# Products on their own PSUM bank, and earlier operands, in a two-layer encoder trunk

## The chip, the cores and the metric

The kernel runs on one core of a Trainium2 chip. The metric is device microseconds (us) of one execution. The kernel before takes 1584.87 us, the median of 3 runs (1580.16 to 1585.47).

## The reference

A stream of 16 learned meta tokens and 512 frames, 1024 wide, goes through two layers in float32. Cut to what matters:

```python
h = concat(meta, x)                                        # 528 tokens
h = h + retention_mixer(rmsnorm(h), w_in, gn, w_o)         # layer 0: 4 heads, chunks of 64
h = h + (silu(n @ w1) * (n @ w3)) @ w2                     # n = rmsnorm(h); w1, w3: 1024x2816
kv_a = rmsnorm(h, g_kv) @ w_kv_a                           # 512 latent + 64 rotary key
k, v = up-projection of rmsnorm(kv_a[:512]) @ w_kv_b       # 8 heads, 128 + 64 rotary; v 128
q = rope(rmsnorm(rmsnorm(h) @ w_q_a) @ w_q_b)              # rank 768, 8 heads
h = h + (softmax(mask(q k^T)) @ v) @ w_o                   # block-causal, chunks of 64
h = h + (silu(n @ w1') * (n @ w3')) @ w2'                  # layer 1's feed-forward
return rmsnorm(h)[frames]
```

## The kernel before

**Layout and precision.** Activations lie transposed, features on the 128 partitions and tokens along the row: 528 of them (`T`) in the first layer and in the keys and values, 512 in the second layer's query side and feed-forward. Each operand is split in a high and a low half: `split` is a ScalarE copy (L316) and a VectorE subtraction (L312, the line of every `tt`), and `weights` does it for a block of weights that SyncE (SP) loads. Each product is three matmuls (high·high, high·low, low·high).

**Feed-forward** (`ffn`, `quads`; 76 quads). A 2x2 block product is done with seven products instead of eight. A *quad* is one such block with tokens cut in halves of `w` = 264 or 256 columns: an `Up` makes a pair of column blocks of w1 and w3 (12 matmuls a product), a `Down` adds one of four parts of w2 into the stream (3 matmuls for each of its `size` hidden pairs; `PARTS`, L48, lists the sizes). A layer has 38 quads, 8 Up, 4 Down (part 0), 8 Up, 4 Down, 6 Up, 4 Down, 4 Down. The products Q1 to Q7 accumulate in the four banks of one PSUM tile, `b0` or `b1`, in turn (L918). Sums of products are formed where they lie: ScalarE copies a bank into another (L833) before a product is added to it, and copies Q5's bank into `q5` (L887); `combine` (VectorE) adds q5 to two banks; `mid`, `act` and `fin` finish. In an Up, `mid` and `fin` multiply by 1/rms and by SiLU; in a Down they add to `h`, and in the last part of layer 1 also the squares for the final norm.

`period(i)` (L855) overlaps quad `i` (`q`), the one before (`prev`) and the loads of the next two; the order in which it issues is forced on every engine (L908 to L913). TensorE's order in it is Q1(q), Q7(prev), Q3(prev), Q5(q), Q6(q), Q4(prev), Q2(q). Four combinations of weights are made per quad: SP loads four parts raw (`load1` to `load4`), GpSimd adds with two accumulating DMAs (L801, L804), VectorE subtracts (`sum2` L807, `sum4`), and `group` splits two at a time: r1 for Q1 and Q5, r2 for Q6 and Q2, r3 for Q7 and Q3, and `group4` one for Q4. `hidden(i)` makes the next Down operand (`operands`, L760) in two halves in two successive periods, as `room` allows. `start` in period 0 takes the layer's root of the mean square.

**Second layer's attention** (`mla`, L977). First `prep_mla(k)` for each of 8 blocks of `h`: the scaled, split operands of the key-value branch and of the query branch, and a square added to a sum; then `gemm` of w_kva (5 blocks of 48 matmuls, first 528 columns), then w_qa, the first keys, values and queries. Eight heads follow; each has four blocks of scores, softmax and one `values`. Between a head's steps a `Filler` issues steps of other projections, in the order of the dictionary `order`, as many as `FILL` (L56) says: `query` (qN), `keys_values` (kvN, two heads), `rotary`, `project` (pN, output projection of two heads). Tiles come from a pool of slots (`MLA_SLOTS`, L46) and PSUM has four tiles for all of it (`pp`). After the last `project` the pools are shut, new ones opened, and `prep_ffn(1, k)` for 8 blocks makes the operands of layer 1's feed-forward.

```python
def product(q, bank, p, first):          # L824; the matmul is L829
nc.scalar.copy(out=q.q5, in_=q.ps[:, 3, :w])             # L887
for k in range(KD): self.prep_ffn(1, k)                  # in run(), after mla
```

Of the kernel before, what the change touches and what calls it, by code (L numbers as in the profile page):

```python
# [19 lines left out]
P = 128  # L20
D = 1024
# [23 lines left out]
RET_SLOTS = 45  # L45
MLA_SLOTS = 53  # L46

PARTS = (3, 3, 3, 2)  # L48

# [39 lines left out]
class Head:  # L89


    def __init__(self, k, n, kn, v, vi, qn, qr, krh, krl):
        self.k, self.nc = k, k.nc
# [53 lines left out]
    def values(self):  # L147
        k, nc = self.k, self.nc
        po = k.ps()
        c = slice(self.vi * P, (self.vi + 1) * P)  # L150
        for j in range(4):
            vh, vl = (u[:, c] for u in self.v[j])
            q0 = min(j, 2) * P
            ph, pl = (z[j // 2][:, j % 2, q0:] for z in (self.ph, self.pl))
            for t, (x, y) in enumerate(((vh, ph), (vh, pl), (vl, ph))):
                nc.tensor.matmul(po[:, q0:SEQ], x, y, start=j == 0 and t == 0, stop=False)  # L156
        nc.tensor.matmul(po[:, :SEQ], self.v[4][:, c], self.pm[:, :SEQ], start=False, stop=True)
        hi, lo = k.slot(F32R), k.slot(F32R)
        k.split(hi[:, :SEQ], lo[:, :SEQ], po[:, :SEQ])
        return hi, lo  # L160


class Quad:
# [7 lines left out]

    def mid(self, c1):
        pass
# [8 lines left out]
class Up(Quad):  # L182
# [11 lines left out]

    def mid(self, c1):
        self.t = self.k.temp()
        self.k.tt(self.two(self.t), c1, self.two(self.k.r), ALU.mult)

# [15 lines left out]
class Down(Quad):  # L214
# [12 lines left out]

    def add(self, i, c, op):
        k, h = self.k, self.h(i)
        k.tt(h, *((c, h) if op == ALU.add else (h, c)), op)  # L230
        if self.done and not self.full:
            m = 2 * self.o + i
            k.square_add(k.acc[:, :SEQ], k.h[m][:, META:], m == 0)

    def mid(self, c1):
        self.add(0, c1, ALU.add)

    def fin(self, c2):
        self.add(1, c2, ALU.subtract)


class Kernel:
# [112 lines left out]

    def gemm(self, src, m0, nm, x, full, chunk_k=8, evac=None, mid=None, mid_at=0):


        nk = len(x)
        for m in range(m0, m0 + nm):  # L360
            ps = self.ps()
            for k0 in range(0, nk, chunk_k):
                k1 = min(nk, k0 + chunk_k)
                hi, lo = self.weights(src[m][:, k0 * P : k1 * P], (k1 - k0) * P)
# [56 lines left out]
    def run(self):  # L421
# [19 lines left out]
        self.shut("pp", "yp")  # L441
        self.ffn(0, True)
        self.metas("mm", 4)
        self.pp = self.pool("pp", bufs=4, space=PSUM)
        self.sp = self.pool("sp", bufs=MLA_SLOTS)
        self.mla()
        self.shut("pp", "sp", "mm")
        self.wx = self.pool("wx")
        self.xp = self.pool("xp", bufs=4)
        for k in range(KD):  # L450
            self.prep_ffn(1, k)
        self.ffn(1, False)
# [11 lines left out]

    def prep(self, k, name, acc, full):

        v = self.h[k] if full else self.h[k][:, META:]
        n = T if full else SEQ
        hi, lo = self.slot(F32R), self.slot(F32R)
        self.split_scaled(hi[:, :n], lo[:, :n], v, self.g(name, k))  # L470
        if acc is not None:
            self.square_add(acc[:, :n], v, k == 0)
        return hi, lo

    def prep_ffn(self, layer, k):
# [10 lines left out]
        if k % 2:  # L486
            self.x.extend(self.operands(self.xp, self.vv, n // 2))

    def prep_mla(self, k):
        if k == 0:  # L490
            self.x, self.xq = [], []
        self.x.append(self.prep(k, "kv", self.acc, True))
        self.xq.append(self.prep(k, "mix1", None, False))

    def retention(self):
# [22 lines left out]
        for k in range(KD):  # L518
            c = slice(k % 4 * P, (k % 4 + 1) * P)
            x.append(self.prep(k, "mix0", None, True))  # L520
            for ps, z in zip(pk + pq, w):
# [254 lines left out]
    def quads(self, seq, w, start, hidden):  # L776
# [47 lines left out]
        def product(q, bank, p, first):  # L824
            wt = q.f[p]
            for k, xp in enumerate(q.xs()):
                cs = slice(k * P, (k + 1) * P)
                for i, (u, v) in enumerate(((0, 0), (0, 1), (1, 0))):
                    nc.tensor.matmul(q.ps[:, bank, :w], wt[u][:, cs], xp[:, p, v, :w], start=first and k == 0 and i == 0,  # L829
                                     stop=False, skip_group_check=True)  # L830

        def copy(q, to, of):
            nc.scalar.copy(out=q.ps[:, to, :w], in_=q.ps[:, of, :w])  # L833

# [17 lines left out]
        def combine(q):  # L852
            self.tt(q.ps[:, 1::2, :w], q.ps[:, 1:3, :w], q.q5[:, None, :].to_broadcast([P, 2, w]), ALU.add)

        def period(i):  # L855
            q, nxt, far = (seq[j] if j < len(seq) else None for j in range(i, i + 3))
            prev = seq[i - 1] if i else None
            if q:
                q.ps = self.pp4[i % 2]
                product(q, 0, Q1, True)  # L860
                group(q, q.r2, Q6, Q2)
                if far:
                    load1(far)
                copy(q, 1, 0)
            if prev:
# [3 lines left out]
                hidden(i)  # L869
                product(prev, 2, Q7, False)  # L870
                product(prev, 1, Q3, False)
                combine(prev)
                prev.mid(prev.ps[:, 0:2, :w])
            if nxt:
                sum2(nxt)
            if q:
# [4 lines left out]
                if nxt:  # L881
                    sum4(nxt)
                product(q, 3, Q5, True)
                if i == 0:
                    start()
                q.q5 = self.temp()[:, :w]
                nc.scalar.copy(out=q.q5, in_=q.ps[:, 3, :w])  # L887
            if nxt:
# [3 lines left out]
            if q:  # L892
                product(q, 1, Q6, False)
                copy(q, 2, 1)
            if prev:
                prev.act()
                product(prev, 2, Q4, False)
                prev.fin(prev.ps[:, 2:4, :w])
            if far:
                add3(far)  # L900
            if q:
                product(q, 0, Q2, False)

# [11 lines left out]
    def ffn(self, layer, full):  # L915
        nc, a = self.nc, self.a
        pool = self.pool("bk", bufs=1, space=PSUM)
        self.pp4 = [pool.tile([P, 4, 512], F32, tag=f"b{i}", name=f"b{i}_{layer}") for i in range(2)]  # L918
        w = HT if full else SEQ // 2
        n = 2 * w  # L920

        for z in self.pp4:
            for j in (1, 2):
                nc.tensor.matmul(z[:, j, :w], self.ones_r, self.x[0][:, 0, 0, :w], start=True, stop=False,
# [12 lines left out]
        def start():  # L937
            root(self.pp4[1][:, 3])
            nc.scalar.activation(out=acc, in_=r[:, :n], func=AF.Copy, scale=-1.0)
# [5 lines left out]
        for part, size in enumerate(PARTS):  # L945
# [4 lines left out]
            if part == 2:  # L950
                room += [(self.xp, len(seq) + 1)] * PARTS[3]
            for o in range(KD // 2):
# [15 lines left out]
        if not full:  # L968
            root(self.pp4[0][:, 0])
            for k in range(KD):  # L970
# [6 lines left out]
    def mla(self):  # L977
        nc, a = self.nc, self.a
        for k in range(KD):
            self.prep_mla(k)  # L980
        acc, xkv, xq = self.parted(self.acc, True), self.x, self.xq
        r = self.r
# [24 lines left out]
        def evac_q(m, ps):  # L1007
# [4 lines left out]

        drain(self.gemm(a["w_kva"], 0, 5, xkv, True, evac=evac_kv,
                        mid=partial(self.rstd, r, acc, D, self.eps_rms[:, 0:1], True)))
        ckv, cq = [], []
# [23 lines left out]
        def keys_values(pr):  # L1039
# [3 lines left out]
            for i in range(2):  # L1043
                ps = self.ps()
                for k in range(4):
                    c = slice((i * 4 + k) * P, (i * 4 + k + 1) * P)
                    self.mm(ps, (whi[:, c], wlo[:, c]), ckv[k], k == 0, k == 3, True)
                hi, lo = self.slot(F32R), self.slot(F32R)
                self.split(self.two(hi), self.two(lo), self.halves(ps))
# [22 lines left out]
        def project(pairs, g):  # L1072
# [4 lines left out]
            for m in range(4 * g, 4 * g + 4):  # L1077
# [6 lines left out]
                hv = self.h[m][:, META:]  # L1084
                self.tt(hv, ps[:, :SEQ], hv, ALU.add)
                yield

# [5 lines left out]
        for i, _ in enumerate(norm):  # L1093
            if i % 2:
# [54 lines left out]
    def mla_values(self, pr, ckv, out):  # L1149

        w = self.weights(self.a["w_kbv"][pr])
        w = [[u[:, k * 256 : (k + 1) * 256] for u in w] for k in range(4)]
        v = [(self.slot(F32R), self.slot(F32R)) for _ in range(2)]
        for j in range(5):
# [122 lines left out]
```

## Time and profile before

| | |
|---|---|
| median of 3 runs | 1584.87 us |
| profiled execution | 1589.51 us |
| its span, first to last instruction | 1587.5 us |
| mean granted TensorE clock | 0.973 of full |
| layer 0's retention; its feed-forward | to 477; 477 to 868 |
| second layer's attention; its feed-forward | 868 to 1165; to the end |

PE is the matmul engine TensorE, PEld its weight loads, DVE VectorE, ACT ScalarE, POOL GpSimd, SP SyncE. A row of a timeline has a start in us, the mean duration of one instruction in us, engine, line and operation, output<-input by the program's names, shapes, the count that is taken together, and in brackets the idle time before and what released it. An instruction's duration holds more than its turn: the next often starts before its end, so prices of a chain are read from start to start.

### The profile page before, as it was taken

The numbers are of one execution on the slowest core, as the hardware profiler recorded it, in microseconds if no ns is written. First come the engines' busy times: TensorE is split into PE (matmuls) and PEld (weight loads), VectorE is DVE, ScalarE is ACT, GpSimd is POOL, SyncE is SP. The second block draws the span as 40 slices with busy tenths as digits, with TensorE's granted clock in tenths as the row PEclk, the third lists the DMA queues.
The fourth block names the chain that finished last, engine by engine and source line by source line (L and its number), as shares of the span: only waits on it lengthen the run. The fifth ranks groups of instructions, "written<-read, shape, count | busy, mean of one in ns | idle before, by whom it ended". The sixth has DMA issues, their size and how long they took to land. (4 is left out here: it accounts for less than half of the span.)

```text
span 1587.5 us, 27865 instructions
## 1 busy us (share of the span) xinstructions
PE 1460.8 (92%) x10988; PEld 1388.9 (87%) x10988; DVE 1180.5 (74%) x1825; ACT 774.6 (49%) x1365; POOL 152.4 (10%) x196
## 2 busy tenths in 40 slices
PE   8999999999988999999997999989969999999984
PEld 8999999999977999999986988878859998989974
DVE  7585484575595888878888677676786878878876
ACT  6452442433464555545546446555464555545543
POOL 2000000000001111111111000000011111111110
PEclk9999999999998999999999899999979999999997
DMA  6222222132134667667655223212135676676651
GB/s 212 74 69 92 63 94 68 66 93 81 54 86 112 167 145 183 152 166 177 157 128 152 68 92 100 60 47 64 51 85 136 156 169 171 150 179 175 147 122 67
DMA packets 84802, 183.87 MB, mean 116 GB/s; under 512 B 9776, under 2 KB 30384, under 8 KB 84672
## 3 DMA queue, kind: packets, MB, share of 16 engines
q1 hardware_dynamic: 60336, 141.13, 28.2%
q0 software_dynamic: 24336, 40.98, 15.6%
q8 instruction: 86, 1.41, 0.4%
q14 instruction: 44, 0.36, 0.1%
HBM read 178.65 MB, written 2.10 MB: 114 GB/s over the span
## 5 line engine op out<-in xcount | busy, mean ns | idle before, releaser
L829 PE MATMUL b<-xp,whi 128*128 128x264 f32 (+1 forms) x3696 | 699.6, 290 | 77.8 <-ACT t L887 54.7
L829 PEld LDWEIGHTS b<-xp,whi 128*128 128x128 f32 x3696 | 579.4, 192 | 106.2 <-ACT t L887 71.2
L316 ACT CAST whi<-raw 128x1024 fp32r<-128x1024 f32 (+5 forms) x428 | 364.8, 856 | 403.0 <-PE b L829 197.6
L829 PE MATMUL b<-xp,wlo 128*128 128x264 f32 (+1 forms) x1848 | 528.0, 286 | 5.4 <-DVE wlo L312 5.4
L312 DVE TENSOR_TENSOR wlo<-raw,whi 128x1024 fp32r<-128x1024 f32 (+5 forms) x428 | 418.0, 980 | 120.5 <-ACT whi L316 116.8
L829 PEld LDWEIGHTS b<-xp,wlo 128*128 128x128 f32 x1848 | 354.4, 192 | 5.6 <-DVE wlo L312 5.6
L352 PE MATMUL ps<-s,whi 128*128 128x264 f32 x1824 | 303.9, 289 | 12.4 <-ACT whi L316 6.8
L352 PEld LDWEIGHTS ps<-s,whi 128*128 128x128 f32 x1824 | 258.2, 192 | 14.7 <-ACT whi L316 6.8
L352 PE MATMUL ps<-s,wlo 128*128 128x264 f32 x912 | 187.8, 288 | 0.0
L352 PEld LDWEIGHTS ps<-s,wlo 128*128 128x128 f32 x912 | 143.8, 192 | 0.1
L801 POOL DMA_DIRECT2D raw<-w x76 | 66.0, 868 | 772.4 <-DMA raw<-w 373.7
L354 PE MATMUL ps<-s,whi 128*128 128x512 f32 x368 | 117.3, 400 | 2.2 <-DVE s L312 1.4
L622 PE MATMUL ps<-whi,s 128*128 128x256 f32 x640 | 116.2, 281 | 0.4 <-DVE s L312 0.4
L833 ACT COPY b<-b 128x264 f32<-128x264 f32 (+1 forms) x152 | 54.7, 360 | 120.0 <-PE b L829 119.8
L312 DVE TENSOR_TENSOR s<-ps,s 128x256 fp32r<-128x256 f32 (+4 forms) x96 | 51.9, 558 | 73.0 <-ACT s L316 51.5
L622 PEld LDWEIGHTS ps<-whi,s 128*128 128x128 f32 x640 | 99.1, 188 | 0.9 <-DVE s L312 0.7
L804 POOL DMA_DIRECT2D raw<-w x76 | 65.7, 864 | 276.5 <-DMA raw<-w 167.9
L622 PE MATMUL ps<-wlo,s 128*128 128x256 f32 x320 | 89.5, 280 | 0.0
L354 PEld LDWEIGHTS ps<-s,whi 128*128 128x128 f32 x368 | 67.0, 188 | 17.7 <-DVE s L312 2.3
L312 DVE TENSOR_TENSOR xp<-e,xp 128x256 fp32r<-128x256 f32 (+5 forms) x90 | 68.1, 786 | 7.2 <-ACT xp L316 7.2
L354 PE MATMUL ps<-s,wlo 128*128 128x512 f32 x184 | 72.6, 395 | 0.0
L312 DVE TENSOR_TENSOR b<-b,t 128x528 f32<-128x528 f32 (+1 forms) x76 | 53.5, 704 | 24.8 <-PE b L829 24.8
(151 smaller groups left out, 1548.8 us busy)
## 6 DMA issues: line engine op xcount, KB each, us to landing
raw<-w SPq DMA_DIRECT2D x140, 256.0 KB, 3.8
raw<-w SPq DMA_DIRECT2D x44, 512.0 KB, 4.9
raw<-w POOLq DMA_DIRECT2D x88, 256.0 KB, 5.1
raw<-w SPq DMA_DIRECT2D x72, 192.0 KB, 3.2
raw<-w SPq DMA_DIRECT2D x24, 384.0 KB, 3.8
raw<-w POOLq DMA_DIRECT2D x48, 192.0 KB, 3.8
raw<-w_v SPq DMA_DIRECT2D x16, 512.0 KB, 3.8
raw<-w_g SPq DMA_DIRECT2D x16, 512.0 KB, 3.4
```

The costliest lines, as they stand in the source:

```text
L312: self.nc.vector.tensor_tensor(out=out, in0=a, in1=b, op=op)
L316: self.nc.scalar.copy(out=hi, in_=src)
L352: mm(ps[:, h * 512 : h * 512 + HT], w[p], x[q][:, h * HT : (h + 1) * HT], start=s, stop=e)
L354: mm(ps[:, :SEQ], w[p], x[q], start=s, stop=e)
L622: mm(ps[:, :256], x[k][p][:, c], w[k][q], start=k == 0 and i == 0, stop=k == last and i == 2)
L801: nc.gpsimd.dma_start(out=q.r1[:, 1], in_=q.part(3), accum_op=ALU.add)
L804: nc.gpsimd.dma_start(out=q.r3[:, 0], in_=q.part(0), accum_op=ALU.add)
L829: nc.tensor.matmul(q.ps[:, bank, :w], wt[u][:, cs], xp[:, p, v, :w], start=first and k == 0 and i == 0, stop=False, skip_group_check=True)
L833: nc.scalar.copy(out=q.ps[:, to, :w], in_=q.ps[:, of, :w])
```

## The change

In the feed-forward: the first product's bank becomes a tile of its own (`a{i}`), the other three (`b`, `d`, `c`) one tile; the order on TensorE becomes Q1(q), Q7(prev), Q3(prev), Q5(q), Q2(q), Q6(q), Q4(prev), with Q2 now accumulating in the first bank after the copy out of it; `mid` becomes two instructions, one for each bank; `PARTS` becomes (3, 3, 2, 3), with the room of the last two operands unchanged in number.

In attention: the first weights of w_kva are made ahead, then the key-value operands of all 8 blocks, then the squares; the query branch's operands are made two blocks at a time between w_kva's blocks. `yp`, a pool of 8 slots, holds first four query-branch operands, then keys and values of pair 0, then values of heads 2 and later; the common pool has 45 slots for 53. The fillers have another order. The pools of layer 1's feed-forward are opened before the last two projections, and each of their steps that completes a block of `h` calls `prep_ffn` for it.

```diff
-MLA_SLOTS = 53
+MLA_SLOTS = 45
...
-PARTS = (3, 3, 3, 2)
+PARTS = (3, 3, 2, 3)
...
# Head.values
-        hi, lo = k.slot(F32R), k.slot(F32R)
+        pool = k.yp if self.n >= 2 else None
+        hi, lo = k.slot(F32R, pool), k.slot(F32R, pool)
...
# Up.mid; Down.mid likewise
-    def mid(self, c1):
+    def mid(self, c11, c12):
         self.t = self.k.temp()
-        self.k.tt(self.two(self.t), c1, self.two(self.k.r), ALU.mult)
+        for i, c in enumerate((c11, c12)):
+            cs = slice(i * self.w, (i + 1) * self.w)
+            self.k.tt(self.t[:, cs], c, self.k.r[:, cs], ALU.mult)
...
# run
+        self.yp = self.pool("yp", "right", 8)
...
-        self.shut("pp", "sp", "mm")
-        self.wx = self.pool("wx")
-        self.xp = self.pool("xp", bufs=4)
-        for k in range(KD):
-            self.prep_ffn(1, k)
+        self.shut("pp", "yp")
         self.ffn(1, False)
...
# quads
-            self.tt(q.ps[:, 1::2, :w], q.ps[:, 1:3, :w], q.q5[:, None, :].to_broadcast([P, 2, w]), ALU.add)
+            self.tt(q.ps[:, 0::2], q.ps[:, 0:2], q.q5[:, None, :].to_broadcast([P, 2, w]), ALU.add)
...
# period(i)
-                q.ps = self.pp4[i % 2]
-                product(q, 0, Q1, True)
+                a, ps = self.banks[i % 2]
+                q.a, (q.b, q.d, q.c), q.ps = a[:, :w], (ps[:, j, :w] for j in range(3)), ps[:, :, :w]
+                product(q, q.a, Q1, True)
                 group(q, q.r2, Q6, Q2)
...
-                copy(q, 1, 0)
+                nc.scalar.copy(out=q.b, in_=q.a)
...
-                product(prev, 2, Q7, False)
-                product(prev, 1, Q3, False)
+                product(prev, prev.d, Q7, False)
+                product(prev, prev.b, Q3, False)
                 combine(prev)
-                prev.mid(prev.ps[:, 0:2, :w])
+                prev.mid(prev.a, prev.b)
...
-                product(q, 3, Q5, True)
+                product(q, q.c, Q5, True)
                 if i == 0:
                     start()
                 q.q5 = self.temp()[:, :w]
-                nc.scalar.copy(out=q.q5, in_=q.ps[:, 3, :w])
+                nc.scalar.copy(out=q.q5, in_=q.c)
...
-                product(q, 1, Q6, False)
-                copy(q, 2, 1)
+                product(q, q.a, Q2, False)
+                product(q, q.b, Q6, False)
+                nc.scalar.copy(out=q.d, in_=q.b)
             if prev:
                 prev.act()
-                product(prev, 2, Q4, False)
-                prev.fin(prev.ps[:, 2:4, :w])
+                product(prev, prev.d, Q4, False)
+                prev.fin(prev.ps[:, 1:3])
             if far:
                 add3(far)
-            if q:
-                product(q, 0, Q2, False)
...
# ffn
-                room += [(self.xp, len(seq) + 1)] * PARTS[3]
+                room += [(self.xp, len(seq) + 1)] * 2
...
# mla
-            self.prep_mla(k)
+        first = [self.weights(a["w_kva"][0])]
+        xkv = [self.prep(k, "kv", True) for k in range(KD)]
+        xq = []
+        for k in range(KD):
+            self.square_add(self.acc, self.h[k], k == 0)
...
+        for m, _ in enumerate(self.gemm(a["w_kva"], 0, 5, xkv, True, evac=evac_kv, ready=first,
+                                        mid=partial(self.rstd, r, acc, D, self.eps_rms[:, 0:1], True))):
+            for k in range(2 * m, min(2 * m + 2, KD)):
+                xq.append(self.prep(k, "mix1", False, self.yp if k < 4 else None))
...
# project, after the sum into h
+                if 3 in pairs:
+                    self.prep_ffn(1, m)
...
-        order = {"q2": query(2), "kv2": keys_values(2), "q3": query(3), "r1": rotary(1), "q4": query(4),
-                 "p0": project([0], 0), "p0b": project([0], 1), "q5": query(5), "kv3": keys_values(3), "q6": query(6),
+        order = {"q2": query(2), "q3": query(3), "r1": rotary(1), "q5": query(5), "p0": project([0], 0),
+                 "p0b": project([0], 1), "kv2": keys_values(2), "q4": query(4), "kv3": keys_values(3), "q6": query(6),
                  "q7": query(7), "p1": project([1], 0), "p1b": project([1], 1), "p2": project([2], 0)}
...
         filler.until("p2")
+        self.shut("sp", "mm")
+        self.wx = self.pool("wx")
+        self.xp = self.pool("xp", bufs=4)
         drain(project([3], 0))
         drain(project([2, 3], 1))
```

## Rows read from the trace of the kernel before

**Rows 1.** The page, part 1: busy us (share of span) and instructions, by engine.
```profile
PE 1460.8 (92%) x10988; PEld 1388.9 (87%) x10988; DVE 1180.5 (74%) x1825; ACT 774.6 (49%) x1365; POOL 152.4 (10%) x196
```

**Rows 2.** Who waited for whom: total us, times, longest.
```profile
PE b L829 <- ACT t L887: 54.7, 76, 5.0
```

**Rows 3.** Timeline of TensorE, two periods of layer 0 (640 to 664).
```profile
640.49 0.40 PE L829 MATMUL b<-xp,whi 128*128 128x264 f32 x2
...
646.21 0.29 PE L829 MATMUL b<-xp,wlo 128*128 128x264 f32 x1
...
647.02 0.51 PE L829 MATMUL b<-xp,whi 128*128 128x264 f32 x2 [0.52 <-ACT t L887]
...
651.74 0.51 PE L829 MATMUL b<-xp,whi 128*128 128x264 f32 x2
...
662.89 0.40 PE L829 MATMUL b<-xp,whi 128*128 128x264 f32 x2
```

**Rows 4.** Timeline of VectorE in the first of these periods.
```profile
643.07 0.69 DVE L312 TENSOR_TENSOR wlo<-raw,whi 128x512 fp32r<-128x512 f32 x1 [0.20 <-ACT whi L316]
643.68 1.04 DVE L312 TENSOR_TENSOR xp<-e,xp 128x528 fp32r<-128x528 f32 x2
...
646.14 0.71 DVE L312 TENSOR_TENSOR b<-b,t 128x528 f32<-128x528 f32 x1
646.89 0.71 DVE L312 TENSOR_TENSOR t<-b,r 128x528 f32<-128x528 f32 x1
647.51 0.68 DVE L807 SCALAR_TENSOR_TENSOR raw<-raw 128x512 f32<-128x512 f32 x1
648.11 1.22 DVE L312 TENSOR_TENSOR wlo<-raw,whi 128x1024 fp32r<-128x1024 f32 x1
649.25 0.68 DVE L312 TENSOR_TENSOR raw<-raw 128x512 f32<-128x512 f32 x1
649.85 1.22 DVE L312 TENSOR_TENSOR wlo<-raw,whi 128x1024 fp32r<-128x1024 f32 x1
650.98 0.70 DVE L312 TENSOR_TENSOR t<-b,t 128x528 f32<-128x528 f32 x1
```

**Rows 5.** Timeline of ScalarE in the same period: the copy of line 887.
```profile
646.59 0.38 ACT L887 COPY t<-b 128x264 f32<-128x264 f32 x1 [0.59 <-PE b L829]
```

**Rows 6.** VectorE's groups with shapes, 633 to 797: busy us, mean ns; idle.
```profile
L312 DVE TENSOR_TENSOR t<-b,r 128x528 f32<-128x528 f32 x12 | 8.5, 708 | 0.4
...
L312 DVE TENSOR_TENSOR e<-e,e 128x264 f32<-128x264 f32 x10 | 4.3, 429 | 0.2
```

**Rows 7.** Windows: stretch, us; busy of PE, PEld, DVE, ACT, POOL; clock, DMA, GB/s.
```profile
797.55:868.30 70.75, 60.55 (x458) 56.68 (x456) 58.11 (x97) 39.23 (x73) 12.34 (x15) 1.00 0.55 138
...
1494.79:1570.60 75.81, 61.45 (x458) 57.99 (x456) 57.18 (x95) 35.75 (x70) 11.22 (x13) 0.95 0.41 95
...
683.49:691.98 8.49, 7.97 (x65) 7.76 (x64) 6.89 (x10) 3.94 (x7) 1.73 (x2) 1.00 0.67 163
...
868.00:885.20 17.20, 11.58 (x53) 10.33 (x53) 16.97 (x27) 11.44 (x20) 0.54 (x1) 0.60 0.25 76
...
987.00:1166.00 179.00, 167.89 (x995) 143.57 (x993) 127.92 (x325) 97.71 (x254) 5.69 (x10) 0.99 0.21 61
```

**Rows 8.** Timeline of VectorE, layer 1, where a Down gives way to an Up.
```profile
1313.98 0.69 DVE L807 SCALAR_TENSOR_TENSOR raw<-raw 128x512 f32<-128x512 f32 x1 [1.81 <-DMA raw<-w]
```

**Rows 9.** Timeline of TensorE, last Downs of layer 1: Q6.
```profile
1554.49 0.51 PE L829 MATMUL b<-xp,whi 128*128 128x256 f32 x2 [2.25 <-ACT t L887]
```

**Rows 10.** Timeline of TensorE from attention's last matmul into layer 1.
```profile
1164.91 0.39 PE L354 MATMUL ps<-s,wlo 128*128 128x512 f32 x1
...
1179.99 0.58 PE L829 MATMUL b<-xp,whi 128*128 128x256 f32 x1 [1.21 <-DVE xp L312]
...
1188.30 0.79 PE L829 MATMUL b<-xp,whi 128*128 128x256 f32 x2 [4.87 <-ACT t L887]
```

**Rows 11.** Who waited for whom, TensorE in attention, 987 to 1166.
```profile
PE ps L156 <- ACT t L124: 2.9, 1, 2.9
```

More of the change, by code (lines that the diff above doesn't have):

```diff
@@ L92, in __init__ @@
     def __init__(self, k, n, kn, v, vi, qn, qr, krh, krl):
-        self.k, self.nc = k, k.nc
+        self.k, self.nc, self.n = k, k.nc, n
         self.kn, self.v, self.vi, self.qn, self.qr, self.krh, self.krl = kn, v, vi, qn, qr, krh, krl
@@ L193, in two, with mid @@
         return z[:, : 2 * self.w].rearrange("p (h c) -> p h c", h=2)
-    def mid(self, c1):
+    def mid(self, c11, c12):
         self.t = self.k.temp()
-        self.k.tt(self.two(self.t), c1, self.two(self.k.r), ALU.mult)
+        for i, c in enumerate((c11, c12)):
+            cs = slice(i * self.w, (i + 1) * self.w)
+            self.k.tt(self.t[:, cs], c, self.k.r[:, cs], ALU.mult)
     def act(self):
@@ L226, in h, with squares, mid @@
         return (z if self.full else z[:, META:]).rearrange("p (h c) -> p h c", h=2)
-    def add(self, i, c, op):
-        k, h = self.k, self.h(i)
-        k.tt(h, *((c, h) if op == ALU.add else (h, c)), op)
+    def squares(self, i):
         if self.done and not self.full:
             m = 2 * self.o + i
-            k.square_add(k.acc[:, :SEQ], k.h[m][:, META:], m == 0)
-    def mid(self, c1):
-        self.add(0, c1, ALU.add)
+            self.k.square_add(self.k.acc[:, :SEQ], self.k.h[m][:, META:], m == 0)
+    def mid(self, c11, c12):
+        h = self.h(0)
+        self.k.tt(h[:, 0], c11, h[:, 0], ALU.add)
+        self.k.tt(h[:, 1], c12, h[:, 1], ALU.add)
+        self.squares(0)
     def fin(self, c2):
-        self.add(1, c2, ALU.subtract)
+        h = self.h(1)
+        self.k.tt(h, h, c2, ALU.subtract)
+        self.squares(1)
 class Kernel:
@@ L354, in mm, with gemm @@
                 mm(ps[:, :SEQ], w[p], x[q], start=s, stop=e)
-    def gemm(self, src, m0, nm, x, full, chunk_k=8, evac=None, mid=None, mid_at=0):
+    def gemm(self, src, m0, nm, x, full, chunk_k=8, evac=None, mid=None, mid_at=0, ready=()):
         nk = len(x)
@@ L363, in gemm @@
                 k1 = min(nk, k0 + chunk_k)
-                hi, lo = self.weights(src[m][:, k0 * P : k1 * P], (k1 - k0) * P)
+                if ready:
+                    hi, lo = ready.pop(0)
+                else:
+                    hi, lo = self.weights(src[m][:, k0 * P : k1 * P], (k1 - k0) * P)
                 for k in range(k0, k1):
@@ L463, in metas, with prep @@
             self.nc.vector.memset(z.bitcast(F32), 0.0)
-    def prep(self, k, name, acc, full):
+    def prep(self, k, name, full, pool=None):
         v = self.h[k] if full else self.h[k][:, META:]
         n = T if full else SEQ
-        hi, lo = self.slot(F32R), self.slot(F32R)
+        hi, lo = self.slot(F32R, pool), self.slot(F32R, pool)
         self.split_scaled(hi[:, :n], lo[:, :n], v, self.g(name, k))
-        if acc is not None:
-            self.square_add(acc[:, :n], v, k == 0)
         return hi, lo
@@ L487, in prep_ffn @@
             self.x.extend(self.operands(self.xp, self.vv, n // 2))
[L489 to L493, printed above, removed]
     def retention(self):
@@ L519, in retention @@
             c = slice(k % 4 * P, (k % 4 + 1) * P)
-            x.append(self.prep(k, "mix0", None, True))
+            x.append(self.prep(k, "mix0", True))
             for ps, z in zip(pk + pq, w):
@@ L828, in product @@
                 for i, (u, v) in enumerate(((0, 0), (0, 1), (1, 0))):
-                    nc.tensor.matmul(q.ps[:, bank, :w], wt[u][:, cs], xp[:, p, v, :w], start=first and k == 0 and i == 0,
+                    nc.tensor.matmul(bank, wt[u][:, cs], xp[:, p, v, :w], start=first and k == 0 and i == 0,
                                      stop=False, skip_group_check=True)
-        def copy(q, to, of):
-            nc.scalar.copy(out=q.ps[:, to, :w], in_=q.ps[:, of, :w])
         def begin():
@@ L917, in ffn @@
         pool = self.pool("bk", bufs=1, space=PSUM)
-        self.pp4 = [pool.tile([P, 4, 512], F32, tag=f"b{i}", name=f"b{i}_{layer}") for i in range(2)]
+        self.banks = [(pool.tile([P, 512], F32, tag=f"a{i}", name=f"a{i}_{layer}"),
+                       pool.tile([P, 3, 512], F32, tag=f"b{i}", name=f"b{i}_{layer}")) for i in range(2)]
         w = HT if full else SEQ // 2
         n = 2 * w
-        for z in self.pp4:
-            for j in (1, 2):
+        for _, z in self.banks:
+            for j in (0, 1):
                 nc.tensor.matmul(z[:, j, :w], self.ones_r, self.x[0][:, 0, 0, :w], start=True, stop=False,
@@ L937, in start @@
         def start():
-            root(self.pp4[1][:, 3])
+            root(self.banks[1][0])
             nc.scalar.activation(out=acc, in_=r[:, :n], func=AF.Copy, scale=-1.0)
@@ L968, in ffn @@
         if not full:
-            root(self.pp4[0][:, 0])
+            root(self.banks[0][0])
             for k in range(KD):
@@ L978, in mla @@
         nc, a = self.nc, self.a
+        first = [self.weights(a["w_kva"][0])]
+        xkv = [self.prep(k, "kv", True) for k in range(KD)]
+        xq = []
         for k in range(KD):
-            self.prep_mla(k)
-        acc, xkv, xq = self.parted(self.acc, True), self.x, self.xq
+            self.square_add(self.acc, self.h[k], k == 0)
+        acc = self.parted(self.acc, True)
         r = self.r
@@ L1011, in evac_q @@
             self.square_add(qacc[:, :SEQ], z[:, :SEQ], m == 0)
-        drain(self.gemm(a["w_kva"], 0, 5, xkv, True, evac=evac_kv,
-                        mid=partial(self.rstd, r, acc, D, self.eps_rms[:, 0:1], True)))
+        for m, _ in enumerate(self.gemm(a["w_kva"], 0, 5, xkv, True, evac=evac_kv, ready=first,
+                                        mid=partial(self.rstd, r, acc, D, self.eps_rms[:, 0:1], True))):
+            for k in range(2 * m, min(2 * m + 2, KD)):
+                xq.append(self.prep(k, "mix1", False, self.yp if k < 4 else None))
         ckv, cq = [], []
@@ L1047, in keys_values @@
                     self.mm(ps, (whi[:, c], wlo[:, c]), ckv[k], k == 0, k == 3, True)
-                hi, lo = self.slot(F32R), self.slot(F32R)
+                hi, lo = (self.slot(F32R, None if pr else self.yp) for _ in range(2))
                 self.split(self.two(hi), self.two(lo), self.halves(ps))
@@ L1152, in mla_values @@
         w = [[u[:, k * 256 : (k + 1) * 256] for u in w] for k in range(4)]
-        v = [(self.slot(F32R), self.slot(F32R)) for _ in range(2)]
+        pool = None if pr else self.yp
+        v = [(self.slot(F32R, pool), self.slot(F32R, pool)) for _ in range(2)]
         for j in range(5):
```

## The prediction

> **What bounds the kernel now.** The page comes first: TensorE is busy 92% of the span [rows 1], so an edit pays only where it takes idle time or slow clock from TensorE. Who waited for whom comes next [rows 2]: one wait stands out, TensorE on ScalarE's copy of line 887, 76 times, once for each of the 76 quads of the two feed-forward layers. The timeline of two neighbouring periods of the first layer shows it from near [rows 3 to 5]; I number a layer's periods as `period(i)` does. One starts at 640.49, the next at 651.74. Q5's last matmul starts at 646.21, and Q6, whose slot was 0.12 us later (12 matmuls of a product take 1.46, so one takes 0.121), starts at 647.02: 0.69 us lost, and 0.11 more until the steps are short again. The copy that it waits for starts at 646.59 and lasts 0.38 [rows 5]. It reads the bank of Q5, while Q6 writes another bank of the same tile. So an access anywhere in the tile holds up the tile's next writer. The same explains why Q1 at 651.74 begins just as `fin`'s first subtraction (650.98, 0.70 long) is done [rows 4], though the two touch different banks.
>
> In the Trainium skill (PSUM — Partial Sum Buffer, section "PSUM bank collisions raise a hardware error") engines must be kept apart by bank and quadrant, and two on different banks run clean. By that rule neither wait is the chip's; both are bookkeeping by tile, which a tile of its own ends. If instead the copy's wait has another cause, the new order may not cover it; that is the third rival.
>
> **The change, part by part.**
>
> *Order of products.* After it TensorE runs Q1, prev.Q7, prev.Q3, Q5, Q2, Q6, prev.Q4. Q2 writes the new single-bank tile, whose last reader is the copy after Q1, three products earlier: it starts at once. Q6 still waits for the copy of Q5, but behind Q2: 1.46 us of cover in an Up (1.10 with the 9 matmuls of a Down of size 3, 0.73 at size 2) against a need of 0.69. The next Q1 writes the other single-bank tile, last read by `mid`; it no longer waits for `fin`, which now delays only ScalarE's copy into bank b, with a whole product in front. What is late next is VectorE: Q1 of the next quad needs the low half of its weights (`group` of r1), which VectorE makes last before `fin`.
>
> *VectorE in a period.* Its steps, from one start to the next in [rows 4]: weights of Q7 and Q3 1.14, and so those of Q6 and Q2; group4 0.61; `operands`, first half, 2.46 (643.68 to 646.14), second half about 1.2 (one split of 1056 columns); combine 0.75; mid 0.62; sum2 0.60; sum4 0.60; weights of Q1 and Q5 1.13; fin 1.44 (two of 0.70, each waiting for the one before, as mid waits for combine). `mid` becomes two instructions: one of 528 columns lasts 0.708, one of 264 lasts 0.43 [rows 6], so it gains 0.15 in durations; in steps I take 0.13, between that and 0.10 (two steps of 0.36). In a heavy period (first half of `operands`) fin starts 0.26 in, as long after Q4's slot as the copy of line 887 after Q5's, and 0.26 + 1.44 + 1.14 + 0.61 + 2.46 + 0.75 + 0.75 + 0.60 + 1.14 + 0.60 + 1.22 ends at 10.97. TensorE, streaming 84 matmuls, reaches Q1's third matmul, the first to need the low half, at 10.20 + 0.24: a stall of 0.55 and 0.12 of restart, 10.87 in all. In a light period VectorE's sum is 1.3 less and fits: 10.20. The pair takes 21.07 where it took 662.89 - 640.49 = 22.40: 1.33 less. There are seven such pairs a layer: 14 x 1.33 = 18.6.
>
> *Other Up periods* (five a layer: no first half, or a Down next) lose the stall of 0.80 and a tenth at Q1: 10 x 0.9 = 9.0. *Down of size 3*: 8.49 [rows 7] falls to 63 x 0.121 = 7.65; six a layer (two of them with an Up behind), 12 x 0.8 = 9.6.
>
> *Down to Up, twice a layer.* DMAs are late there already: sum2 waited 1.81 us for its accumulating DMA [rows 8], and a chain of DMAs doesn't shorten when the engines do. Of the 1.6 that the stalls of two periods would give I take 0.6: 4 x 0.6 = 2.4 (bounds 0 and 6.4).
>
> *PARTS (3, 3, 2, 3).* Periods 30 to 38 took 70.75 and 75.81 [rows 7]. The Downs of size 2 now stand where `operands` of the last two pairs are made. Layer 0: period 30 is 60 matmuls, 7.3. Periods 31 to 34 are paced by VectorE, with the steps above halved for size 2 (period 31: 1.44 + 0.6 + 0.34 + 2.46 + 0.75 + 0.75 + 0.34 + 0.6 + 0.34 + 0.6 = 8.2): 8.2 + 6.1 + 7.9 + 7.2. Periods 35 to 37 are 63 matmuls, 7.65 each; the tail is 27 matmuls, 3.3, and a wait for combine, 2.4. Together 65.4, a gain of 5.3. Layer 1 adds the squares: there Q6 waits 2.25 us behind ScalarE's Square, which waits for `mid` [rows 9]. At size 3 that chain starts nine matmuls later and is 0.4 longer, and `fin`'s square adds as much at the head of the next period: 9.3 a period, 69.3 in all, a gain of 6.5. Together 11.8 (bounds 4 and 18).
>
> *Starts of the layers.* In period 0 Q6 waits 4.87 us behind the root's reciprocal [rows 10]; Q2 moves into that wait, at half clock 2.7 us, in both layers: 5.4. The second layer's operands: before, their last split lets Q5's last operand go at 1179.99, while attention's last matmul starts at 1164.91 [rows 10]. That looks like 14 us to win, but VectorE is the queue there, and it gets the same work in another order; only weight splits that stood ahead of the last operand, and small idle bits, go: 2.5 (bounds 1 and 10). Together 7.9.
>
> *Start of MLA.* The 17.2 us from 868.0 hold 53 matmuls, at clock 0.60, with VectorE busy 16.97 [rows 7]: for each k it makes the operands of both branches and adds a square. After the change only the eight low halves of the first branch stand ahead of the first block's 48 matmuls; the other eight and the additions lie beside the 192 matmuls of the next blocks. The first block then ends some 4.2 sooner (bounds 2 and 6), its first half still at the slow clock.
>
> *Attention.* It takes 179.0 us from 987.0, of which TensorE is idle 11 [rows 7]. The fillers change their order under the old step counts: heads 1 and 2 lose the keys and values of pair 2 as filler (pair 0 can't be projected before head 1's values), these come in one block before head 4, and head 7's end has none left. A softmax without cover costs up to 2.9 [rows 11]; I count five more waits of 1.6: +8. The pool of slots falls from 53 to 45, with 8 beside it; by my count of the code `rotary(1)` asks for eight when about five are free, and until it has them its two results hold two of the four PSUM tiles. Bounds: -3 and +30; I take +8, nearest the rows.
>
> **Sum.** 18.6 + 9.0 + 9.6 + 2.4 + 11.8 + 7.9 + 4.2 - 8 = 55.5. The profiled execution took 1589.51 with a span of 1587.5, and would take 1534.0. The median of the runs is 1584.87, 4.6 below it: 1584.87 - 55.5 = 1529.4.
>
> **The rivals.**
> *VectorE paces all of it.* For: in a heavy period its durations add up to over 11 us. Against: the steps in [rows 4] are a tenth shorter than the durations. Each pair would take 21.5 instead of 21.07 (+6), and periods 31 to 37 a tenth more (+9): 1544.
> *Attention loses more.* For: the slots above. Against: the block before head 4 leaves later heads more filler. At +25: 1546.
> *It doesn't do what it says.* If Q2 too waits for the copy of Q5, the gains in pairs, Ups and Downs (37) go: 1567. Against: it writes another tile.
> *Slower.* Place: heads 0 to 3. `rotary(1)` sits on two of four PSUM tiles, a query's result on a third, and every score, transpose and value product goes through what is left. A head takes 179 / 8 = 22.4 us; if three and a bit run at half pace that is +72 in place of 8: 1593. It decides from 63 us, nearly three heads. For: the count of slots. Against: a score needs one tile only, and each head that is done gives slots back.
> *Better.* Attention loses nothing and the heavy stall (14 x 0.67) is hidden: 1529.4 - 8 - 9.4 = 1512.
>
> **Chances.** Forecast 0.54; VectorE 0.12; attention 0.13; better 0.12; not what it says 0.03; starved heads 0.06, a third of it within 0.3% (about what a measurement of this kernel can tell from no change), the rest slower. Faster 0.94, same 0.02, slower 0.04. The range, 1508 to 1556, holds the forecast, the first two rivals and the last with the bounds of their terms.
>
> **What would show it.** TensorE's wait for line 887's copy falls from 55 us to a few, left in the last periods of layer 1; in Ups, Q1 starts 10.9 and 10.2 us apart in turn, released by VectorE's low half and not by `fin`; Down periods take 7.7; the first MLA block is done 4 us sooner; TensorE is idle more in heads 1, 2 and 7. The prediction is wrong if Q6 still waits in Ups, if VectorE's low half holds up light periods too, or if attention, from its first score to the second layer's first matmul, takes over 200 us.

## The result, and the profile after

The changed kernel takes 1547.41 us, the median of 4 runs (1544.75 to 1550.03), against 1584.05 (1580.16 to 1585.47): a ratio of 0.9772 [0.9747, 0.9798], 36.6 us less. 55.5 were forecast. The two profiled executions differ by 43.0 (1589.51 and 1546.48); the one of before lies 5.5 above its median, the one of after 0.9 below. The sums below are those of the traces, taken between the starts of Q1; a minus is time gained:

| stretch | forecast | before | after | change |
|---|---|---|---|---|
| Ups, 38 periods | -27.6 | 422.1 | 391.7 | -30.4 |
| Downs of size 3, 12 periods | -9.6 | 105.0 | 95.1 | -9.9 |
| Down to Up, 4 times two periods | -2.4 | 77.3 | 84.6 | **+7.3** |
| periods 30 to 38, both layers | -11.8 | 146.2 | 140.0 | **-6.2** |
| starts of the layers | -7.9 | 54.5 | 45.0 | -9.5 |
| start of MLA, to the first score | -4.2 | 118.6 | 115.8 | -2.8 |
| attention, first score to last matmul | +8 | 178.3 | 186.9 | +8.6 |

Busy time by engine, to be set beside [rows 1], and who waited for whom on TensorE, beside [rows 2] (total us, times, longest). In this kernel line 827 is the matmul of `product`, 318 VectorE's `tt`, 322 ScalarE's high half:

```profile
PE 1442.9 (93%) x10988; PEld 1388.2 (90%) x10988; DVE 1170.7 (76%) x1901; ACT 768.0 (50%) x1365; POOL 152.3 (10%) x196
```

```profile
PE a L827 <- DVE wlo L318: 21.9, 19, 5.4
PE b L827 <- ACT t L883: 10.7, 6, 3.5
PE b L827 <- DVE h L318: 10.2, 6, 1.9
...
PE b L920 <- DVE h L318: 6.3, 2, 4.3
PE a L827 <- ACT whi L322: 5.0, 3, 1.9
```

The wait for the copy of Q5 (now line 883) fell from 54.7 us and 76 times to 10.7 and 6. What is late now is VectorE's low half of the next quad's weights. Two neighbouring Up periods of layer 0 on TensorE, as in [rows 3]:

```profile
510.19 0.41 PE L827 MATMUL a<-xp,whi 128*128 128x264 f32 x2
...
520.43 0.41 PE L827 MATMUL a<-xp,whi 128*128 128x264 f32 x2
520.94 0.39 PE L827 MATMUL a<-xp,wlo 128*128 128x264 f32 x1
...
531.03 0.41 PE L827 MATMUL a<-xp,whi 128*128 128x264 f32 x2
```

The periods take 10.24 and 10.60 in turn, 20.84 for the pair that took 22.40. Q1's third matmul, the first on the low half, comes at 520.94 where 520.67 was its turn.

A layer's quads run 8 Up, 4 Down, 6 Up, 4 Down, 8 Up and then 8 Down; the section on the kernel before has the 6 and the last 8 Ups the wrong way round. A junction is the last Down period and the first Up period behind it. At the second junction of layer 0 (last Down of part 1 to the Up numbered 14, U14; periods 21 and 22) TensorE now stops twice, for the high and then for the low half of Q1's weights; before it is what it waits for, SP's load and GpSimd's accumulating DMA for U14, and VectorE's `sum2`:

```profile
690.26 0.51 PE L827 MATMUL a<-xp,whi 128*128 128x264 f32 x2 [1.88 <-ACT whi L322]
692.52 0.59 PE L827 MATMUL a<-xp,wlo 128*128 128x264 f32 x1 [1.75 <-DVE wlo L318]
692.90 0.64 PE L827 MATMUL a<-xp,whi 128*128 128x264 f32 x2
```

```profile
674.66 0.33 SPq L784 DMA_DIRECT2D raw<-w  x1
```

```profile
681.62 0.87 POOL L799 DMA_DIRECT2D raw<-w  x1 [6.45 <-DVE h L318]
```

```profile
689.17 0.69 DVE L805 SCALAR_TENSOR_TENSOR raw<-raw 128x512 f32<-128x512 f32 x1 [3.73 <-DMA raw<-w]
```

The load is issued at 674.66 and lands at 681.0. The accumulating DMA is issued 0.6 later (the row names `h` as its releaser, but it follows the load's landing by 0.6 at each junction) and lands at 689.1. [rows 8] showed the like before, a wait of 1.81 for the next Up's accumulating DMA. After the stop three matmuls take 0.66 instead of 0.37 for 3 us: the clock is at its lower level (0.86 over the period, below).

Windows of after (stretch, us; busy of PE, PEld, DVE, ACT, POOL; clock, DMA share, GB/s): the junction's two periods, periods 31 to 34 and 35 to 38 of layer 0, MLA's start and attention, beside [rows 7]. In attention TensorE is idle 15.6 us where it was idle 11.1, and its clock is 0.96 where it was 0.99.

```profile
680.54:690.26 9.72, 7.84 (x65) 7.63 (x63) 4.61 (x8) 3.38 (x7) 2.12 (x3) 1.00 0.73 177
690.26:702.84 12.58, 10.83 (x76) 10.62 (x77) 9.37 (x13) 5.22 (x9) 2.20 (x3) 0.86 0.71 168
...
782.83:814.41 31.58, 25.20 (x183) 23.92 (x181) 28.55 (x57) 16.60 (x35) 6.90 (x8) 0.95 0.67 150
814.41:843.89 29.48, 27.25 (x218) 26.44 (x216) 24.95 (x40) 18.59 (x33) 2.59 (x3) 1.00 0.60 157
...
843.89:857.57 13.68, 9.01 (x47) 7.95 (x46) 13.45 (x23) 8.10 (x14) 1.64 (x3) 0.75 0.27 96
959.65:1146.00 186.35, 170.71 (x992) 145.86 (x991) 129.55 (x326) 100.70 (x257) 7.39 (x12) 0.96 0.23 63
```

The start of layer 1, beside [rows 10]: TensorE's first matmul there waits 4.29 for VectorE's last sum into `h`; then, with Q2 in front, Q6 waits 3.47 for the copy behind the root, where it waited 4.87.

```profile
1150.80 1.20 PE L920 MATMUL b<-xp,ones_r 128*128 128x256 f32 x4 [4.29 <-DVE h L318]
...
1167.45 0.80 PE L827 MATMUL b<-xp,whi 128*128 128x256 f32 x2 [3.47 <-ACT t L883]
```

### The profile page after: what moved, and what is told of

It is laid out like the page before. It is cut to its first block, busy times and chain, and to the rows that moved or that the text cites. A ratio compares the mean times of both kernels' runs of the same rounds, so it can differ in the third digit from the quotient of the medians.

```text
span 1544.5 us, 27868 instructions
## 1 busy us (share of the span) xinstructions
PE 1442.9 (93%) x10988; PEld 1388.2 (90%) x10988; DVE 1170.7 (76%) x1901; ACT 768.0 (50%) x1365; POOL 152.3 (10%) x196
## 3 DMA queue, kind: packets, MB, share of 16 engines
q0 software_dynamic: 24336, 40.98, 15.6%
## 5 line engine op out<-in xcount | busy, mean ns | idle before, releaser
L827 PE MATMUL b<-xp,whi 128*128 128x264 f32 (+1 forms) x2640 | 493.7, 287 | 23.2 <-ACT t L883 10.7
L318 DVE TENSOR_TENSOR wlo<-raw,whi 128x1024 fp32r<-128x1024 f32 (+5 forms) x428 | 413.8, 977 | 61.2 <-ACT whi L322 59.1
L827 PEld LDWEIGHTS b<-xp,whi 128*128 128x128 f32 x2640 | 414.9, 192 | 26.7 <-ACT t L883 11.9
L827 PE MATMUL b<-xp,wlo 128*128 128x264 f32 (+1 forms) x1320 | 376.6, 285 | 0.0
L358 PE MATMUL ps<-s,whi 128*128 128x264 f32 x1824 | 303.2, 288 | 11.1 <-ACT whi L322 6.5
L358 PEld LDWEIGHTS ps<-s,whi 128*128 128x128 f32 x1824 | 256.9, 191 | 13.4 <-ACT whi L322 6.5
L827 PEld LDWEIGHTS b<-xp,wlo 128*128 128x128 f32 x1320 | 253.0, 192 | 0.0
L827 PE MATMUL a<-xp,whi 128*128 128x264 f32 (+1 forms) x1056 | 204.4, 289 | 5.0 <-ACT whi L322 5.0
L358 PE MATMUL ps<-s,wlo 128*128 128x264 f32 x912 | 187.2, 287 | 0.0
L827 PE MATMUL a<-xp,wlo 128*128 128x264 f32 (+1 forms) x528 | 156.3, 296 | 22.7 <-DVE wlo L318 21.9
L827 PEld LDWEIGHTS a<-xp,whi 128*128 128x128 f32 x1056 | 168.2, 194 | 5.7 <-ACT whi L322 5.6
L827 PEld LDWEIGHTS a<-xp,wlo 128*128 128x128 f32 x528 | 102.9, 195 | 29.0 <-DVE wlo L318 28.7
```

The lines of the kernel that those rows point to most:

```text
L318: self.nc.vector.tensor_tensor(out=out, in0=a, in1=b, op=op)
L358: mm(ps[:, h * 512 : h * 512 + HT], w[p], x[q][:, h * HT : (h + 1) * HT], start=s, stop=e)
L827: nc.tensor.matmul(bank, wt[u][:, cs], xp[:, p, v, :w], start=first and k == 0 and i == 0, stop=False, skip_group_check=True)
```

## The experiments

Stretches are named and measured as in the table. The kernel before, run beside them on the same chip, had medians of 1584.1 to 1585.6.

**The feed-forward edits alone.** The kernel before, with own tile, new order and `mid` in two.

> The kernel before with the feed-forward edits alone (own tile for the first bank, new order of products, mid in two); PARTS (3, 3, 3, 2), attention and the making of layer 1's operands as before. Theory 1 (the terms of the changed kernel add up from separate parts): Ups give 30, Downs of size 3 10, the two period 0 together 5 to 7, Down-to-Up junctions lose 7, the last nine periods give 4 to 8: about 1540 (1536 to 1546), with attention at 178 us from first score to last matmul. Rival: the junction loss and a part of the gain hang on PARTS or on when layer 1's operands come; then it stays above 1550 or falls under 1535.

Measured: 1535.84 (1533.65 to 1537.09), ratio 0.970 [0.9682, 0.9718]. It is 11.6 us faster than the whole change and just under the range of theory 1. Ups 392.1 and Downs 95.1 are those of after, junctions lose 4.8, attention takes 178.1. But periods 30 to 38 take 64.3 and 68.6, where after takes 68.5 and 71.5. So theory 1 was too low there (13.4 for 4 to 8): what I credited to PARTS the order brings, and PARTS takes part of it back.

**The same order on one tile, and the own tile with the old order.** Against the run above, shortened:

```diff
# order_one_tile
- a{i} = pool.tile([P, 512]), b{i} = pool.tile([P, 3, 512])
+ z = pool.tile([P, 4, 512]); a, b = z[:, 0], z[:, 1:]
# tile_old_order
- product(q, q.a, Q2); product(q, q.b, Q6); ... Q4(prev)
+ product(q, q.b, Q6); ... Q4(prev) ...; product(q, q.a, Q2)
```

> As ffn_only, but the four banks are one tile again, as in the kernel before; the order of products is the new one. Theory 1 (a wait goes by tile, not by bank): Q2 takes over Q6's wait for ScalarE's copy of Q5, and Q1 now follows Q4 at once and waits for fin's first subtraction, about 1.0 us in each of 76 periods, as no product lies between them any more: slower than before, 1620 to 1660. Rival (the waits come from the engines' timing, not from the tile): within 5 us of ffn_only.

> As ffn_only, but the order of products is that of the kernel before (Q6 straight behind Q5, Q2 last); the first bank keeps its own tile. Theory 1: TensorE's wait for the copy of Q5 stays (50 to 57 us in sum), and only Q1's short wait for fin goes, 0.1 us a period: 1572 to 1584. Rival (the own tile is what pays, whatever the order): within 10 us of ffn_only.

Measured: 1652.56 (1651.04 to 1653.58) and 1565.99 (1563.62 to 1567.52). TensorE's waits with one tile, then with the old order, and last in the run with the feed-forward edits alone, which has both (line 834 is the matmul, 890 the copy of Q5, 317 `tt`):

```profile
PE b L834 <- ACT t L890: 54.8, 76, 5.0
PE b L834 <- DVE t L317: 40.4, 44, 1.7
PE b L834 <- DVE h L317: 31.4, 30, 2.8
```

```profile
PE b L834 <- ACT t L890: 54.5, 76, 5.0
```

```profile
PE b L834 <- ACT t L890: 11.7, 6, 3.5
```

With one tile both waits stand: Q2's for the copy of Q5 in all 76 periods, and Q1's for `fin` (`t` in the Ups, `h` in the Downs) in 72, though each pair touches different banks. This settles that the wait goes by tile: the same banks in two tiles don't wait. It agrees with the Trainium skill (PSUM — Partial Sum Buffer, section "PSUM bank collisions raise a hardware error"), by which engines on different banks run clean. The own tile alone gives 18 us, with `mid` in two, which no run takes apart from it; the order is worth 30 us with the own tile, and on one tile the run is 68 slower than before. The second forecast missed by 6: the own tile also shortens periods 30 to 38 by 8.2 and the junctions by 4.7. Before, Q1 waited for `fin` 9.0 us in 23 periods, 6.8 of it behind Downs; here it waits for it in none, and Ups fall by 8.7 too. A part of these figures is the long profiled execution of before (see the part on why the prediction was right).

**Four raw buffers, and fewer transfers at the junctions.** Both are edits of the changed kernel, shortened here.

```diff
# raw4
- self.wp.tile([P, WC], F32, tag="raw", ...)
+ self.wp.tile([P, WC], F32, tag="raw", ..., bufs=4)
# fewer
  def load4(q):
+     if seq.index(q) in (10, 11, 20, 21): q.r4 = ones; return
  def add3(q):
+     if seq.index(q) in (11, 12, 21, 22): return
```

> The changed kernel with four raw weight buffers in place of three. In its trace the four Down-to-Up junctions (two periods each) take 84.7 us, against 72 if all were as the quickest (7.93 + 10.05): U14's first load starts at 674.7, when a raw buffer comes free, lands at 681.0, its accumulating DMA at 689.1, and Q1 waits for the split behind it. Theory J1 (the load starts too late, for want of a buffer): it starts 2 us sooner, junctions fall to 74 to 80, time 1537 to 1543. Theory J2 (the transfers there are limited by the rate of the DMA engines, an earlier start only stretches them): junctions stay at 82 to 86, time 1545 to 1550.

> The changed kernel with transfers left out around each Down-to-Up junction: no second accumulating DMA for the last Down and the first Up, and no fourth load for the last two Downs (ones stand in for those weights, so these products are not the reference's). The first load of the Up and its accumulating DMA stay, with all that waits for them. Theory J2 (transfers share the DMA engines' rate): these two land in 4 to 5 us each instead of 6.3 and 7.5, junctions fall from 84.7 to 72 to 76, time 1534 to 1540. Rival J3 (the chain of load and accumulating DMA is as long by itself): they land as late as before, junctions stay above 81, time above 1543.

Measured: 1527.22 (1525.12 to 1533.33), ratio 0.9638 [0.9609, 0.9667], and 1531.66 (1529.52 to 1534.94), both under all that was forecast. Junctions fall to 69.4 and 70.4; with four buffers period 0 of layer 0 falls too, from 21.4 to 18.3. SP's load for U14 with four buffers, and the windows of the same two periods:

```profile
670.22 0.33 SPq L784 DMA_DIRECT2D raw<-w  x1
```

```profile
677.98:685.66 7.68, 7.68 (x65) 7.68 (x64) 4.91 (x8) 3.69 (x8) 1.65 (x3) 1.00 0.88 222
685.66:696.63 10.97, 9.42 (x77) 9.21 (x76) 9.07 (x13) 4.92 (x8) 1.92 (x3) 1.00 0.79 186
```

The traces' own times can't be compared as they stand, as with four buffers period 21 starts 2.6 us sooner (677.98 for 680.54). Counted from that start, the load is issued 7.8 us ahead of it instead of 5.9, 1.9 sooner, as J1 said; the accumulating DMA lands 6.3 us behind it instead of 8.6. Load and accumulating DMA take 6.5 and 7.0, hardly less than the 6.4 and 7.5 of after. The rate, 177 GB/s in after, was not at its limit: here it is 222. So J1 holds, with a larger gain than it said, and J2's claim that an earlier start only stretches the transfers falls. With fewer transfers the same two take 4.9 and 6.0 (J3 falls): other transfers in flight do lengthen the chain, so this half of J2 holds beside J1. It is a chain with a deadline, from the freeing of a raw buffer to Q1 two periods later. When the change took some 0.8 us or more out of each Down period it took it out of the chain's time.

**PARTS as before.** The changed kernel with one line undone.

> The changed kernel with PARTS (3, 3, 3, 2) again. Theory P1 (the time of a period is the longer of TensorE's and VectorE's work, so VectorE's operands belong into the longer periods): the last nine periods, 68.5 and 71.5 us in the changed kernel, take 64 to 65 and 68 to 69 as in the run with the feed-forward edits alone; time 1538 to 1543. Theory P2 (what the prediction assumed: the new PARTS keeps operands out of the way of size-3 Downs): the last nine take 70 us or more, time 1549 or more.

Measured: 1537.72 (1535.42 to 1543.08); periods 30 to 38 take 63.5 and 68.4, 8.1 less together, as P1 had it. Windows of periods 31 to 34 and 35 to 38 of layer 0:

```profile
789.51:822.71 33.20, 30.72 (x242) 29.63 (x241) 30.62 (x57) 18.48 (x35) 6.90 (x8) 1.00 0.60 136
822.71:844.20 21.49, 19.04 (x146) 17.98 (x144) 20.65 (x40) 17.16 (x35) 2.58 (x3) 1.00 0.60 172
```

In periods 31 to 34 VectorE has about the same to do (28.6 and 30.6) whatever PARTS is. With size 2 TensorE has 25.2 of work there and waits; with size 3 it has 30.7 and the two overlap in 33.2. The matmuls that were taken out come back in periods 35 to 38, 27.3 instead of 19.0, where VectorE has less to do than TensorE (25.0 in 29.5); with size 2 there the two are even again (20.7 and 19.0 in 21.5).

**Layer 1's operands after the last projections**, as before; the rest of the change stays.

> The changed kernel, but layer 1's operands are made after the last projection, as in the kernel before. Theory O1 (VectorE is the queue there either way): from attention's last matmul to the second period's start it takes 25 to 27 us instead of 23.7, time 1548 to 1551. Theory O2 (the early operands are what shortened the start, 29.2 before): 28 us or more, time 1551 to 1555. Theory O3 (early operands hold up the last projections by as much): time within 1 us of the changed kernel.

Measured: 1550.05 (1544.19 to 1551.32). From attention's last matmul to the second period 23.7, as in after, and attention 187.3: O3. The 2.6 between the medians are less than the spread of either; in the traces the junctions differ by 5.0. O3's 1 us was missed by the median. That the early operands bring nothing beyond these spreads is shown; why the start is still 2 us shorter than with the feed-forward edits alone (25.7) stays open.

**The order of fillers.** On the kernel before, and later on the fastest kernel below, with the 53 slots kept.

> The kernel before with the new order of attention's fillers alone; slots stay 53, everything else as before. Theory A (heads 1 and 2 run out of fillers, whatever the slots): attention, from first score to last matmul, goes from 178 to 184 to 189 us, and the time to 1589 to 1596. Rival B (the loss comes from the 45 slots, for which steps wait): attention stays at 177 to 180 and the time within 2 us of before.

Measured: 1591.90 (1586.46 to 1593.96), ratio 1.0047 [1.0031, 1.0062], attention 181.3. The median says A; the trace, of the shortest of the seven executions, shows 3.0 and not 6. Hence the second run, behind the next two.

**What the runs point to.** Four raw buffers and the old PARTS on the changed kernel (best_a), and on the kernel before with the feed-forward edits and of attention only the new start (best_b).

> The changed kernel with four raw buffers and PARTS (3, 3, 3, 2). If junctions and last periods are separate losses, the sum holds: the run with four buffers (1527.2) less the last nine periods' difference between its trace (141.2) and that with PARTS (3, 3, 3, 2) (131.9): 1518 (1514 to 1522). Rival: with four buffers the Downs of size 2 at the end start a new wait for transfers, and less than half of the 9.3 remains: above 1523.

> The kernel before with the feed-forward edits, four raw buffers, PARTS (3, 3, 3, 2), and of attention's edits only the new start (weights ahead, key-value operands first, query operands within the first product); fillers, 53 slots and late operands as before. Theory S (the rest of attention's edits costs 6 to 9 us in attention and brings some 2 at the second layer's start): ffn_only's 1535.8 less 12.7 at the junctions and 3.3 at attention's start: 1520 (1515 to 1524), within 6 us of best_a either way; attention from first score to last matmul 178 to 180, its start 116. Rival: the pool and the order belong together with the new start, which without them takes 118 or more: 1524 or more.

> As best_b (1513.4, attention 178.3), with the changed kernel's order of fillers; the slots stay 53. The run with that order alone on the kernel before was 7.5 us slower in its median, but its one trace shows 3.0 more in attention. Theory A (the order is all of attention's loss): attention 185 to 188, 1519 to 1523. Theory B (order and slots each have a part): attention 180 to 183, 1515 to 1518, and the rest of the 8.9 us by which best_a's attention is longer belongs to the slots.

Measured: best_a 1521.43 (1517.46 to 1523.57), ratio 0.9602 [0.9584, 0.9621]; best_b **1513.43** (1512.20 to 1516.18), ratio 0.9559 [0.9543, 0.9575], the fastest, 34 us under the changed kernel; with the new order of fillers 1516.46 (1514.46 to 1519.05). Junctions take 67.7 and 67.8. best_a lies in its range: the fourth buffer gives 16.3 with the old PARTS (1537.7 to 1521.4), where it gave 20.2 with the new, and the old PARTS 5.8 by the medians, where the traces' last nine periods differ by 9.6. best_b beat its range: against the feed-forward edits alone the junctions gave 14.3 for the 12.7 expected, attention's start 5.0 for 3.3 (no run has the new start alone), and period 0 of layer 0 fell by 2.1, which I had not counted.

Attention takes 178.3, 181.0 with the order, 187.2 with order and 45 slots (best_a, which also has the early operands, but these made no difference to attention above): theory B. The six traces with 45 slots show 184.7 to 187.3, so the rest, which I put to the slots, is 4 to 6. Of best_a's 6.2, 5.5 lie between the values of head 0 and of head 1 (16.1 for 10.6). There, by the copies of `rotary(1)` on ScalarE in best_a and then with 53 slots (duration in ns, first and last start):

```profile
L1187 ACT CAST s<-s x8: 612/617/619, 973.4 to 989.2; 32x512 fp32r<-32x512 f32 x8
```

```profile
L1182 ACT CAST s<-s x8: 612/617/622, 971.9 to 977.6; 32x512 fp32r<-32x512 f32 x8
```

ScalarE in best_a at the end of these copies:

```profile
987.89 0.62 ACT L1187 CAST s<-s 32x512 fp32r<-32x512 f32 x1 [0.93 <-PE ps L113]
...
990.42 0.70 ACT L124 ACTIVATE t<-ps,mx 128x528 f32<-128x528 f32 x1
```

The last two copies come some 10 us late, and the one shown is released by head 1's scores (L113). Nothing but a slot that comes free links the two in the code, so I read it as that; no run changed the slots alone, so it isn't shown. Head 1's last softmax (L124) queues behind the copies. If that is so, it is the shortage that the slower rival named, at 4 to 6 us instead of 64.

## Why the prediction was right, and where it was wrong

The direction held and the time lay in the range, 18 us above the forecast. The steps that carry it were right: the wait went by tile, Q2 covers the copy of Q5, VectorE's low half is late every other Up, Downs take 7.7. The pair was forecast at 10.87 and 10.20 and took 10.60 and 10.24; two terms together were 3 us too small. By its number the result lies at the rivals with 1544 and 1546, but neither came about: pairs took 20.84 and not 21.5, and attention lost 8.6 and not 25.

**Down to Up** was mis-sized with the wrong sign, the largest miss: I took a gain of 2.4, with bounds of 0 and 6.4, and measured a loss of 7.3. I had said that "a chain of DMAs doesn't shorten when the engines do", and bounded it as if it could at worst give nothing. But it has a deadline counted in periods, and a shorter period brings the deadline nearer; two stops and a stretch at the lower clock follow. The chain also grew: from the issue of the Up's first load to the landing of its accumulating DMA it took 9.5 to 10.9 us at the four junctions before and 11.5 to 14.5 after, but 9.6 to 11.5 with fewer transfers. A loss should have been inside the bounds.

**PARTS** was credited with 11.8, taken from periods of before that still had the old order's stalls; measured 6.2, of which the order gives 13.4 (146.2 to 132.8 with the feed-forward edits alone) and PARTS takes back 7 to 10, by the pair of traces. The nine periods themselves were forecast at 65.4 and 69.3 and took 68.5 and 71.5: in layer 0 periods 31 to 34, said to be paced by VectorE, took 31.6 for 29.4, and the three behind them 24.1 for 23.0. The edit had to be priced against the kernel with all other edits in it.

**Attention** was right in sum (8 longer, measured 8.6), which is luck: the order costs 3 of the 8, and the slots, by the reading above, 4 to 6. The slots were counted as a rival only.

**Starts of layers and of MLA** gave 12.3 for 12.1, by luck too. The early operands, for 2.5, gave nothing, and MLA's start gave 2.8 for 4.2. The feed-forward edits gave more than the 2.7 a layer: alone, 5.0 in layer 0 (1.6 of it the long execution of before, see below) and 3.5 in layer 1. Of this the rows show 1.4 in the wait behind the root; the rest isn't taken apart.

The last 6.4 between 43.0 and 36.6 are not the change's: the profiled execution of before was a long one, and I read the terms from it without allowance. The trace of the run with the new order of fillers on the kernel before, which has the same code outside attention, shows where: layer 0's period 0 takes 23.7 there and not 25.3, Ups 420.7 and not 422.1, junctions 74.9 and not 77.3, the last nine periods 145.5 and not 146.2, 6.1 less together. Against that trace the junctions lose 9.7.

## What to carry to other kernels

Price each edit of a bundle against the kernel with the others in place; two edits that fix the same stall are paid once, and the later one may only cost. When engines get faster, look for chains that start when a buffer comes free and must end a fixed number of steps later: they don't shorten, here they even grew, and one more buffer, 4 KB a partition, was worth 16 to 20 us. Put an engine's long tasks into the periods in which the other engine is long too.

## What the runs showed that was not expected

The same first load of an Up (512 KB) took 4.3 to 6.5 us and its accumulating DMA 4.4 to 7.5 at the junctions of after and of the runs with four buffers and with fewer transfers; with fewer they took 4.3 to 4.9 and 4.7 to 6.0. With three buffers and the new order the length of a junction is a matter of chance, in kernels that are the same up to there: the first of layer 0 took 18.0 us in after, 22.5 with the old PARTS and 24.0 with late operands, while in the four runs with four buffers 15 of 16 junctions took 16.7 to 17.2, and one 18.7.
